# Weight products in runs of six, and score products queued behind the output of the head ahead

## The chip, the cores and the metric

The kernel runs on one core of a Trainium2 chip. The metric is the device time of one execution in microseconds. The engines are named as the profile names them: PE (TensorE), DVE (VectorE), ACT (ScalarE), POOL (GpSimd) and SP (SyncE, whose queue issues the weight loads).

## The reference

One step of a decoder trunk with four layers, for 256 prompt tokens and 8 x 4 sample tokens, which share all weights (288 columns together). Each layer is two half-weighted SwiGLU FFNs around a token mixer:

```
for i in range(4):
    x = x + 0.5 * swiglu(rms(x), ffn_w_in[i, 0], ffn_w_out[i, 0])
    x = x + mixer[i % 3](rms(x))          # 0 attention, 1 gated delta rule, 2 linear recurrence
    x = x + 0.5 * swiglu(rms(x), ffn_w_in[i, 1], ffn_w_out[i, 1])
```

The mixers are sliding-window attention with sinks (layers 0 and 3), a gated delta rule, called GDN here (layer 1), and a gated linear recurrence, HGRN (layer 2). The recurrence, per head of 128 x 128 state and in chunks of 32 tokens, is

```
attn = einsum('bhid,bhjd,bhijd->bhij', qc, kc, decay)
o = einsum('bhik,bhkv->bhiv', qc * exp(bcum), s) + einsum('bhij,bhjv->bhiv', attn, vc)
s = s * exp(bcum[-1]) + einsum('bhjk,bhjv->bhkv', kc * exp(b_last - bcum), vc)
```

followed by an RMS norm of o per head, a gate and the output weights. States of prompt and samples are outputs too. All is fp32.

## The kernel before

**Weight products.** A weight times the 288 columns is made in a form close to fp32: each weight tile is split into a high and a low part (ACT, L71, and DVE, L72, from a raw tile that SP loads, L54), each activation too, and a k-tile takes three matmuls of 128x288 (L97, L98, L99: high by high, high by low, low by high). Class `Stream` holds all weights of the program as a list of jobs in order; `st.run(n)` emits the next n jobs, four k-tiles (12 products) in most. There are 16152 products, in four layers of FFN, mixer, FFN.

**Order.** The kernel is written in an order that does not interleave; a scheduler does that. Each instruction has a priority, its place in the text, and code inside `tc.high_priority(PRIO)` (PRIO is 5000) is moved ahead of it. The mixers' units of small matmuls stand under such a priority, so that the scheduler takes an instruction of a unit when it is due and fills the time between with products. The order per engine is then fixed; an engine waits at its next instruction.

**PSUM.** Eight banks: three `acc` for the products, two `ma`, and one each of `c0`, `c1` and `s` for the mixers' small matmuls. A product that begins a new accumulator needs a free `acc`.

**GDN.** `core_unit` makes for pairs of heads the chunked rule: the inverse of the 64 x 64 triangles (L735 to L877 and on), and then for each chunk in turn L1181 (products with the state), L1182/L1183 on DVE and ACT, L1186 (new values), L1187 on ACT, L1190 and L1192 (state and output), L1195 on DVE, which updates the state that the next L1181 reads. L1140 updates the sample states.

**HGRN.** `run` emits the set-up, 56 jobs of the input weights, then under high priority the heads 0 to 3, eight jobs, heads 4 to 7, eight jobs. The in-projection has 768 products, the out-projection twice 96; the first 96 need the gates of heads 0 to 3. Per head:

- `head_scores(h)`: the state of the head is loaded by SP (two buffers); `factors` multiplies the decays of 2, 4, 8, 16 and 32 tokens (L1366, L1370, DVE); from them the scaled K on DVE and Q on POOL, level by level (L1386 to L1404, tiles `W`, 14 buffers). Then 51 score matmuls of 32x32 in bank c0 (L1415), masks and sums on DVE (L1419 to L1425), block matrices `bd` on POOL (L1427, L1430), and, in c0 again, the transposes of K (L1436, L1437) with a copy on ACT (L1439).
- `head_states(h)`: chunk sums (L1459, banks c1 and s), the chain of states SS on DVE (L1463, L1465), the output `po` in c1 (L1470, L1474, L1478, L1479), its squares on ACT (L1483), mean on DVE (L1485), the inverse square root as a power on POOL (`root`, L276), the scale on ACT (L1488), the sample states (L1492 in s and then c1, L1494 on DVE), and the output's transposes in s (L1499 to L1501).
- `gate(h)`: L1505 on DVE (heads 0 to 3) or POOL, L1506 on ACT, L1507 on DVE.

The heads are called as

```
head_scores(0)
for h in range(a, a + 4):
    if h < 7:
        head_scores(h + 1)
    head_states(h)
    gate(h)
```

Of the kernel before, what the change touches and what calls it, by code (L numbers as in the profile page):

```python
# [15 lines left out]
T = 288  # L16
# [8 lines left out]
class Stream:  # L25
# [3 lines left out]
    def __init__(self, tc, raw, split, psum):  # L29
        self.tc, self.nc, self.raw, self.split_pool, self.psum = tc, tc.nc, raw, split, psum  # L30
        self.chunks, self.jobs = [], []
        self.loaded, self.tiles, self.left = 0, {}, {}
        self.nsplit, self.parts = 0, {}
        self.njob = 0
        self.accs = {}
        self.pooled = set()
        self.held, self.mms, self.tags = [], [], {}
        self.loads = {}
        self.first = 0

# [44 lines left out]
    def run(self, count, hold=False):  # L85
        self.mms = []
        for j in range(self.njob, self.njob + count):
            self.split_to(j + 1 + AHEAD)
            chunk, view, nk, xs, acc, start, stop, evac, m = self.jobs[j]
            hi, lo = self.parts.pop(j)  # L90
            if start:
                self.accs[acc] = self.psum.tile([128, 512], F32, tag=self.tags.pop(acc, "acc"), name="acc")
            ps = self.accs[acc][:m, :T]
            mm = self.nc.tensor.matmul
            last = len(xs) - 1
            for i, (xh, xl) in enumerate(xs):
                mm(ps, hi[:, i, :m], xh(), start=start and i == 0, stop=False)  # L97
                mm(ps, hi[:, i, :m], xl(), start=False, stop=False)  # L98
                self.mms.append(mm(ps, lo[:, i, :m], xh(), start=False, stop=stop and i == last).ins)  # L99
            self.njob += 1  # L100
            if stop and hold:
                self.held.append((evac, self.accs.pop(acc)))
            elif stop:
                evac(self.accs.pop(acc))
# [7 lines left out]
def trunk(ctx: ExitStack, tc: tile.TileContext, I, consts, O):  # L112
# [1168 lines left out]
    def hgrn(i, j):  # L1281
# [91 lines left out]
        def head_scores(h):  # L1373


            kh, qh, fh = k[h], q[h], f[h]
            s0 = slice(32 * (h % 4), 32 * (h % 4) + 32)
# [7 lines left out]
            Q[1] = mx(T, "W", 14)  # L1385
            G.tensor_tensor(out=Q[1], in0=qh, in1=fh, op=ALU.mult)  # L1386
            for s in (2, 4, 8, 16, 32):
                n = T if s <= 4 else 256
                K[s], Q[s] = mx(T, "W", 14), mx(256, "qb", 2) if s == 32 else mx(T, "W", 14)
# [16 lines left out]
            kd, t4 = K[32], four(K[4], "k4t")  # L1406
# [27 lines left out]
            ps = misc("c0")  # L1434
            for c in range(2):
                PE.transpose(ps[:, c * 128:c * 128 + 128], kd[:, c * 128:c * 128 + 128], ident)  # L1436
            PE.transpose(ps[:, 256:384], t4, ident)  # L1437
            H["kdt"] = mx(256, "kdt", 2)
            S.activation(out=H["kdt"], in_=ps[:, 0:256], func=AF.Copy)  # L1439
            H["k4"] = mx(128, "k4", 2, dt=F32R)  # L1440
            hilo(H["k4"], ps[:, 256:384], ((32, 32), (96, 32)))

        def head_states(h):
# [35 lines left out]
            PE.matmul(po[:, 256:384], bd[s0, 256:384], L["vs"][s0, h // 4], start=False, stop=True)  # L1479
# [6 lines left out]
            root(r, v)  # L1486
# [3 lines left out]
            for e in range(0, 8, 4):  # L1490
                ps = misc(("c1", "s")[e // 4])
                PE.matmul(ps, H["k4"], v4m[:, e:e + 4].rearrange("p b v -> p (b v)"))  # L1492
                for a in range(4):
                    V.scalar_tensor_tensor(out=sta[:, e + a], in0=sta[:, e + a], scalar=H["ends"][:, (e + a) // 2, a % 2:a % 2 + 1],  # L1494
                                           in1=ps[:, a * 128:a * 128 + 128], op0=ALU.mult, op1=ALU.add)
            nc.sync.dma_start(out=O[11][j, :, h].rearrange("b k v -> k b v"), in_=sta)
            ps = misc("s")
# [23 lines left out]
        def run():  # L1521
# [3 lines left out]
            for a in (0, 4):  # L1525
                with tc.high_priority(PRIO):
                    if a == 0:
                        head_scores(0)
                    for h in range(a, a + 4):
                        if h < 7:  # L1530
                            head_scores(h + 1)
                        head_states(h)
# [225 lines left out]
```

## Time and profile before

| | |
|---|---|
| time of three runs | 2638.28, 2638.93, 2644.87 us (median 2638.93) |
| the profiled execution | 2632.71 us, span 2630.9 us |
| busy: PE, DVE, ACT, POOL | 2549.8 (97%), 1763.5 (67%), 1414.1 (54%), 246.4 us (9%) |
| mean granted clock of PE | 0.989 |
| DMA | 400.15 MB, mean 152 GB/s |
| stretches of the mixers | layer 0 some 20 to 380, GDN 700 to 1170, HGRN 1600 to 1870, layer 3 2200 to 2440 us |

An "idle before" or a wait names what released the engine. The clock is a share of full speed, so that a stretch of 0.89 has 22% of its time at half speed. In a timeline the duration of a matmul runs to its modelled end, and matmuls overlap: the time of one is the distance from its start to the next start.

### The profile page before, as it was taken

How to read it: one execution, taken by the hardware profiler on the slowest of the kernel's cores; microseconds unless marked ns; L12 is line 12 of the kernel's file. 1: busy time of each engine (PE TensorE's matmuls, PEld its weight loads, DVE VectorE, ACT ScalarE, POOL GpSimd, SP SyncE). 2: the span in 40 equal slices, each digit the busy share in tenths (PEclk: the TensorE clock that was granted, in tenths of full speed). 3: DMA queues.
4: the chain of work that ended last, by engine and by line, in shares of the span. 5: the costliest groups of instructions: out<-in, count | busy, mean ns of one | idle time of the engine just before them, and what ended most of it. 6: DMA issues, size and time to landing. Idle time of an engine off the chain costs nothing.

```text
span 2630.9 us, 52770 instructions
## 1 busy us (share of the span) xinstructions
PE 2549.8 (97%) x20268; PEld 2411.8 (92%) x20268; DVE 1763.5 (67%) x3772; ACT 1414.1 (54%) x3129; POOL 246.4 (9%) x404
## 2 busy tenths in 40 slices
PE   8999999999998899999999999888999999999998
PEld 8999799999997776789999999677999999979998
DVE  6666776576567867667666666877765766667655
ACT  5555655455455456755555545665554555465543
POOL 1000000000002135410000000443000000010000
PEclk9999999999999999999999999999999999999999
DMA  6655245555553354455555555333555565534553
GB/s 188 196 168 172 65 143 164 165 168 161 166 163 97 109 152 136 136 176 159 167 163 163 168 163 160 106 119 122 164 165 164 164 202 177 168 94 121 161 168 124
DMA packets 442609, 400.15 MB, mean 152 GB/s; under 512 B 24730, under 2 KB 440212, under 8 KB 442356
## 3 DMA queue, kind: packets, MB, share of 16 engines
q1 hardware_dynamic: 441732, 395.66, 49.9%
q8 instruction: 159, 2.61, 0.4%
q10 hardware_dynamic: 624, 1.11, 0.1%
q14 instruction: 94, 0.77, 0.1%
HBM read 374.64 MB, written 22.07 MB: 151 GB/s over the span
## 4 chain that ended last, share of the span: by engine, by line
PE 78%; issue 11%; DVE 6%; POOL 2%; ACT 2%; DMA 1%; DVEq 0%; POOLq 0%; ACTq 0%; SPq 0%
PE acc L97 23%; PE acc L99 23%; PE acc L98 23%; DVE lo L72 1%; PE s L545 1%; PE c L530 1%; PE c L1186 0%; DVE W L1400 0%; PE ma L537 0%; PE c L1190 0%; DVE F L1366 0%; PE c L1192 0%; PE c L1181 0%; PE c L1474 0%; ACT hi L71 0%
## 5 line engine op out<-in xcount | busy, mean ns | idle before, releaser
L97 PE MATMUL acc<-sl,hi 128*128 128x288 f32 x5384 | 1612.4, 300 | 13.0 <-ACT sl L1506 2.8
L98 PE MATMUL acc<-sl,hi 128*128 128x288 f32 x5384 | 1606.1, 298 | 1.8 <-DVE sl L1507 1.8
L99 PE MATMUL acc<-sl,lo 128*128 128x288 f32 x5384 | 1600.8, 298 | 2.4 <-DVE lo L72 2.4
L71 ACT ACTIVATE hi<-raw 128x512 fp32r<-128x512 f32 (+1 forms) x1378 | 854.3, 621 | 963.0 <-PE acc L98 934.4
L72 DVE TENSOR_TENSOR lo<-raw,hi 128x512 fp32r<-128x512 f32 (+1 forms) x1378 | 948.4, 689 | 571.2 <-ACT hi L71 515.1
L97 PEld LDWEIGHTS acc<-sl,hi 128*128 128x128 f32 x5384 | 1016.4, 189 | 26.2 <-issue 11.5
L99 PEld LDWEIGHTS acc<-sl,lo 128*128 128x128 f32 x5384 | 1021.2, 190 | 14.6 <-issue 10.0
L98 PEld LDWEIGHTS acc<-sl,hi 128*128 128x128 f32 x5384 | 1018.9, 189 | 12.8 <-issue 9.2
L276 POOL TENSOR_TENSOR r<-v,roots 128x3 f32<-128x3 f32 x5 | 5.8, 1164 | 1847.2 <-DVE v L296 1847.2
L366 DVE TENSOR_TENSOR sil<-acc,sil 128x288 f32<-128x288 f32 x176 | 79.7, 456 | 54.8 <-PE acc L99 51.3
L359 DVE TENSOR_TENSOR sil<-acc,rbc 128x288 f32<-128x288 f32 x176 | 79.6, 456 | 50.1 <-PE acc L99 49.8
L368 DVE TENSOR_TENSOR sl<-sil,sl 128x288 fp32r<-128x288 f32 x176 | 78.9, 452 | 0.0
L360 ACT ACTIVATE sil<-sil 128x288 f32<-128x288 f32 x176 | 77.6, 445 | 2.1 <-DVE sil L359 2.0
L367 ACT ACTIVATE sl<-sil 128x288 fp32r<-128x288 f32 x176 | 77.6, 445 | 0.0
L700 DVE SCALAR_TENSOR_TENSOR acc<-buf,cw,acc 128x312 f32<-128x312 f32 x96 | 59.0, 625 | 11.9 <-ACT acc L698 11.5
L246 ACT ACTIVATE sl<-x,gT 128x288 fp32r<-128x288 f32 x96 | 51.0, 536 | 26.2 <-DVE x L383 15.3
L249 DVE SCALAR_TENSOR_TENSOR sl<-x,gT,sl 128x288 fp32r<-128x288 f32 x96 | 50.5, 530 | 0.1
L262 ACT ACTIVATE sq<-x 128x288 f32<-128x288 f32 x91 | 38.7, 430 | 5.1 <-DVE x L383 5.1
L515 ACT ACTIVATE e<-e,m 128x128 f32<-128x128 f32 (+1 forms) x72 | 32.6, 454 | 16.1 <-DVE m L512 15.8
L1131 POOL TENSOR_TENSOR st<-st,ex 128x512 f32<-128x512 f32 x32 | 37.4, 1190 | 18.1 <-PE ma L1098 18.1
L259 DVE TENSOR_TENSOR ssq<-ssq,sq 128x288 f32<-128x288 f32 x84 | 37.8, 450 | 0.1
L512 DVE CUSTOM_DVE_ANT_0 e<-c,sl,sink 128x128 f32<-128x128 f32 (+1 forms) x72 | 27.8, 418 | 10.6 <-PE c L530 7.7
(435 smaller groups left out, 1823.3 us busy)
## 6 DMA issues: line engine op xcount, KB each, us to landing
raw<-in_ffn_w_in_dram SPq DMA_DIRECT2D x352, 512.0 KB
raw<-in_ffn_w_out_dram SPq DMA_DIRECT2D x128, 512.0 KB
raw<-in_ffn_w_out_dram SPq DMA_DIRECT2D x64, 384.0 KB
raw<-in_gdn_w_in_dram SPq DMA_DIRECT2D x48, 512.0 KB
raw<-in_hgrn_w_in_dram SPq DMA_DIRECT2D x32, 512.0 KB
out_dram<-st SPq DMA_DIRECT2D x24, 512.0 KB
raw<-in_swa_w_in_dram SPq DMA_DIRECT2D x32, 256.0 KB
raw<-in_swa_w_out_dram SPq DMA_DIRECT2D x32, 256.0 KB
```

Of the source, the lines that this page charges most:

```text
L71: self.nc.scalar.activation(out=h, in_=src, func=AF.Copy)
L72: (self.nc.gpsimd if j in self.pooled else self.nc.vector).tensor_tensor(out=l, in0=src, in1=h, op=ALU.subtract)
L97: mm(ps, hi[:, i, :m], xh(), start=start and i == 0, stop=False)
L98: mm(ps, hi[:, i, :m], xl(), start=False, stop=False)
L99: self.mms.append(mm(ps, lo[:, i, :m], xh(), start=False, stop=stop and i == last).ins)
L246: S.activation(out=h[m], in_=x[:, m], func=AF.Identity, scale=g)
L359: V.tensor_tensor(out=t, in0=ps[:, :T], in1=nrm[key]["rbc"], op=ALU.mult)
L360: S.activation(out=t, in_=t, func=AF.Silu)
L366: V.tensor_tensor(out=t, in0=ps[:, :T], in1=t, op=ALU.mult)
L367: S.activation(out=h, in_=t, func=AF.Copy)
L368: V.tensor_tensor(out=l, in0=t, in1=h, op=ALU.subtract)
L700: V.scalar_tensor_tensor(out=a[:, 0:312], in0=b[:, t:t + 312], scalar=cw[:, 32 * t + mt:32 * t + mt + 1], in1=a[:, 0:312], op0=ALU.mult, o ...
```

## The change

Three things. `Stream.run` gives products a priority of their own: of each pair of k-tiles, the first product keeps the place it had, and the other five follow at three times PRIO, above the units, so that products come in runs of six in the whole program. In HGRN, `head_scores` is split: `head_factors(h)` loads the state and makes the factors, for heads 0 and 1 first and for head h + 2 behind head h; `head_scores(h)` makes the transposes of K first and then the scores, and is held on PE behind a given matmul: behind the job `first + 18` for head 0, behind the last output matmul of head h for head h + 1 (`issue_after`). And in `head_states` the root on POOL becomes `rsqrt`, eleven DVE operations with the mean (a bit shift, a subtraction and three Newton steps of three); the sample states are made in two halves, both in bank s, the second in `head_rest` behind the next scores, with the output's transposes, now in c1. The tiles `W` get 20 buffers.

```diff
@@ -34,9 +34,10 @@
         self.pooled = set()
-        self.held, self.mms, self.tags = [], [], {}
+        self.held, self.mms, self.tags, self.ends = [], [], {}, {}
         self.loads = {}
         self.first = 0
+        self.follow = 3 * PRIO
...
@@ -94,9 +95,13 @@
             for i, (xh, xl) in enumerate(xs):
-                mm(ps, hi[:, i, :m], xh(), start=start and i == 0, stop=False)
-                mm(ps, hi[:, i, :m], xl(), start=False, stop=False)
-                self.mms.append(mm(ps, lo[:, i, :m], xh(), start=False, stop=stop and i == last).ins)
+                with self.tc.high_priority(i % 2 * self.follow):
+                    mm(ps, hi[:, i, :m], xh(), start=start and i == 0, stop=False)
+                with self.tc.high_priority(self.follow):
+                    mm(ps, hi[:, i, :m], xl(), start=False, stop=False)
+                    self.mms.append(mm(ps, lo[:, i, :m], xh(), start=False, stop=stop and i == last).ins)
+            self.ends[j] = self.mms[-1]
             self.njob += 1
...
@@ -1370,11 +1375,9 @@
-        def head_scores(h):
+        def head_factors(h):
             kh, qh, fh = k[h], q[h], f[h]
-            s0 = slice(32 * (h % 4), 32 * (h % 4) + 32)
             H = L["h", h] = {}
...
@@ -1382,11 +1385,11 @@
             K, Q = {1: kh}, {}
-            Q[1] = mx(T, "W", 14)
+            Q[1] = mx(T, "W", 20)
             G.tensor_tensor(out=Q[1], in0=qh, in1=fh, op=ALU.mult)
...
                 n = T if s <= 4 else 256
-                K[s], Q[s] = mx(T, "W", 14), mx(256, "qb", 2) if s == 32 else mx(T, "W", 14)
+                K[s], Q[s] = mx(T, "W", 20), mx(256, "qb", 2) if s == 32 else mx(T, "W", 20)
                 if s == 2:
...
@@ -1403,7 +1406,22 @@
                             in1=L["tok8"].rearrange("p (e t) -> p e t", e=8), op=ALU.mult)
-            kd, t4 = K[32], four(K[4], "k4t")
+            H["K"], H["Q"], H["t4"] = K, Q, four(K[4], "k4t")
+        def head_scores(h):
+            kh, qh, H = k[h], q[h], L["h", h]
+            K, Q, kd, t4 = H.pop("K"), H.pop("Q"), None, H.pop("t4")
+            kd = K[32]
+            s0 = slice(32 * (h % 4), 32 * (h % 4) + 32)
+            ps = misc("c0")
+            for c in range(2):
+                PE.transpose(ps[:, c * 128:c * 128 + 128], kd[:, c * 128:c * 128 + 128], ident)
+            PE.transpose(ps[:, 256:384], t4, ident)
+            H["kdt"] = mx(256, "kdt", 2)
+            S.activation(out=H["kdt"], in_=ps[:, 0:256], func=AF.Copy)
+            H["k4"] = mx(128, "k4", 2, dt=F32R)
+            hilo(H["k4"], ps[:, 256:384], ((32, 32), (96, 32)))
             ps = misc("c0")
...
@@ -1431,14 +1449,6 @@
             H["bd"] = bd
-            ps = misc("c0")
-            for c in range(2):
-                PE.transpose(ps[:, c * 128:c * 128 + 128], kd[:, c * 128:c * 128 + 128], ident)
-            PE.transpose(ps[:, 256:384], t4, ident)
-            H["kdt"] = mx(256, "kdt", 2)
-            S.activation(out=H["kdt"], in_=ps[:, 0:256], func=AF.Copy)
-            H["k4"] = mx(128, "k4", 2, dt=F32R)
-            hilo(H["k4"], ps[:, 256:384], ((32, 32), (96, 32)))
...
@@ -1476,25 +1486,34 @@
                 PE.matmul(po[32 * a:32 * a + 32, 256:384], qm[:, 32 * e:32 * e + 32], sta[:, e], start=False, stop=False)
-            PE.matmul(po[:, 256:384], bd[s0, 256:384], L["vs"][s0, h // 4], start=False, stop=True)
+            L["po"] = PE.matmul(po[:, 256:384], bd[s0, 256:384], L["vs"][s0, h // 4], start=False, stop=True).ins
             ssq, v, r = sm(3, "gs"), sm(3, "gv"), sm(3, "gf")
...
             V.tensor_scalar(v, ssq, 1.0 / 128, EPS, ALU.mult, ALU.add)
-            root(r, v)
+            rsqrt(r, v, ssq)
             for c in range(3):
...
                              scale=r[:, c:c + 1])
-            for e in range(0, 8, 4):
-                ps = misc(("c1", "s")[e // 4])
+            L["rest", h] = sta, H, v4m, o
+            sample_states(h, (0,))
+        def sample_states(h, parts):
+            sta, H, v4m = L["rest", h][0:3]
+            for e in parts:
+                ps = misc("s")
                 PE.matmul(ps, H["k4"], v4m[:, e:e + 4].rearrange("p b v -> p (b v)"))
...
                                            in1=ps[:, a * 128:a * 128 + 128], op0=ALU.mult, op1=ALU.add)
+        def head_rest(h):
+            sample_states(h, (4,))
+            sta, H, v4m, o = L.pop(("rest", h))
             nc.sync.dma_start(out=O[11][j, :, h].rearrange("b k v -> k b v"), in_=sta)
-            ps = misc("s")
+            ps = misc("c1")
             for c in range(2):
...
@@ -1525,11 +1544,18 @@
                     if a == 0:
-                        head_scores(0)
+                        head_factors(0)
+                        head_factors(1)
+                        with tc.issue_after(st.ends[first + 18]):
+                            head_scores(0)
                     for h in range(a, a + 4):
+                        head_states(h)
                         if h < 7:
-                            head_scores(h + 1)
-                        head_states(h)
+                            with tc.issue_after(L["po"]):
+                                head_scores(h + 1)
+                        head_rest(h)
+                        if h < 6:
+                            head_factors(h + 2)
                         gate(h)
...
```

Lines move: L97, L98, L99 are L100, L102, L103 in the changed kernel; the core units' L1181, L1186, L1190, L1192 are L1186, L1191, L1195, L1197, and L1140 is L1145. In HGRN L1415 is L1433, L1436 and L1437 are L1419 and L1420, L1459 is L1469, L1470 to L1479 are L1480 to L1489, L1492 is L1507.

TensorE in HGRN, around the scores of the seventh head. Before, the scores (L1415) stand ahead of the output of the head before (L1470 and on, `po`), and the transposes of K behind:

```order
L1415 MATMUL c_22556<-W 32x32 x33
L1415 MATMUL c_22556<-W,sl 32x32 x9
L1415 MATMUL c_22556<-sl 32x32 x9
L1470 MATMUL c_22660<-sl,bd 128x128
L1474 MATMUL c_22660<-SS,qb 32x128 x3
L1470 MATMUL c_22660<-sl,bd 128x128
L1474 MATMUL c_22660<-SS,qb 32x128
L99 MATMUL acc<-sl,lo 128x288
L97 MATMUL acc<-sl,hi 128x288
L98 MATMUL acc<-sl,hi 128x288
L1436 MATMUL c_22618<-cst,W 128x128 x2
L1437 MATMUL c_22618<-cst,k4t 128x128
```

Changed, around the scores of the sixth head: the transposes (L1419, L1420), a run of six and a sample state (L1507) ahead of the scores (L1433). The last output matmul of the head ahead, L1489, stands two rows above:

```order
L1419 MATMUL c_22481<-cst,W 128x128 x2
L1420 MATMUL c_22481<-cst,k4t 128x128
L1353 MATMUL ma<-cst,v 128x128 x2
L100 MATMUL acc<-sl,hi 128x288
L102 MATMUL acc<-sl,hi 128x288
L103 MATMUL acc<-sl,lo 128x288
L100 MATMUL acc<-sl,hi 128x288
L102 MATMUL acc<-sl,hi 128x288
L103 MATMUL acc<-sl,lo 128x288
L1507 MATMUL s<-v4m,k_22133 128x512
L1433 MATMUL c_22491<-W 32x32 x33
L1433 MATMUL c_22491<-W,sl 32x32 x9
```

The scores moved from before the output of the head ahead to behind it, the transposes from behind the scores to before them.

TensorE in GDN, the core unit of a pair of heads before (`co` is the state, `u` the new values, `w` and `km` belong to the sample states):

```order
L1140 MATMUL ma<-w_11998,km 128x256 x4
L98 MATMUL acc<-sl,hi 128x288
L1186 MATMUL c_12407<-u,sl 64x128 x2
L99 MATMUL acc<-sl,lo 128x288
L97 MATMUL acc<-sl,hi 128x288
L1140 MATMUL ma<-w_11998,km 128x256
L1190 MATMUL c_12407<-u 128x128
L1190 MATMUL s<-u 128x128
L1192 MATMUL c_12407<-u,sl 64x128 x2
L1140 MATMUL ma<-w_11998,km 128x256 x3
L98 MATMUL acc<-sl,hi 128x288
L99 MATMUL acc<-sl,lo 128x288
```

Changed, a stretch of the same unit:

```order
L1195 MATMUL c_12407<-u 128x128
L1195 MATMUL s<-u 128x128
L1197 MATMUL c_12407<-u,sl 64x128 x2
L1130 MATMUL ma<-wp,a_11994 128x128 x2
L1145 MATMUL ma<-w_11998,km 128x256 x2
L1186 MATMUL c_12407<-co,sl 64x128 x4
L1145 MATMUL ma<-w_11998,km 128x256 x4
L1191 MATMUL c_12407<-u,sl 64x128 x2
L1145 MATMUL ma<-w_11998,km 128x256 x2
L1195 MATMUL c_12407<-u 128x128
L1195 MATMUL s<-u 128x128
L1197 MATMUL c_12407<-u,sl 64x128 x2
```

Products that stood between the steps of the unit stand ahead of it and behind it; in this stretch the steps follow each other.

## Rows read from the trace of the kernel before

**Rows 1.** The page: the span, and the chain that ended last by engine.

```profile
span 2630.9 us, 52770 instructions
...
PE 78%; issue 11%; DVE 6%; POOL 2%; ACT 2%; DMA 1%; DVEq 0%; POOLq 0%; ACTq 0%; SPq 0%
```

**Rows 2.** Stretches: width, busy time of five engines, PEclk, DMA share, GB/s.

```profile
20.00:380.00 360.00, 356.97 (x2679) 338.16 (x2678) 243.64 (x577) 193.61 (x421) 13.92 (x23) 0.99 0.51 152
400.00:450.00 50.00, 50.00 (x377) 50.00 (x376) 31.69 (x55) 25.62 (x47) 0.00 (x0) 1.00 0.55 164
700.00:1170.00 470.00, 442.08 (x3848) 374.22 (x3847) 327.13 (x827) 269.43 (x750) 129.39 (x243) 0.98 0.48 138
...
1600.00:1870.00 270.00, 240.85 (x2438) 209.81 (x2437) 208.17 (x477) 164.66 (x456) 83.85 (x109) 0.97 0.42 128
```

**Rows 3.** Waits of PE, 1640 to 1850 us: total, times, longest.

```profile
PE c L1415 <- DVE W L1400: 5.7, 4, 3.0
PE c L1415 <- POOL W L1400: 5.5, 2, 2.9
PE c L1436 <- DVE at L1422: 3.9, 4, 1.4
PE s L1499 <- ACT o L1488: 2.9, 7, 0.5
```

**Rows 4.** Stretches, PE alone: width, busy time, PEclk, DMA share, GB/s.

```profile
1640.00:1670.00 30.00, 23.07 (x332) 0.89 0.28 86
1740.00:1750.00 10.00, 6.18 (x133) 0.87 0.39 112
1830.00:1850.00 20.00, 16.14 (x99) 0.83 0.32 104
850.00:950.00 100.00, 87.70 (x978) 0.91 0.44 121
950.00:1160.00 210.00, 200.67 (x1603) 1.00 0.52 147
```

**Rows 5.** Timeline of PE behind the gates of HGRN: start, duration, instruction.

```profile
1835.17 0.44 PE L97 MATMUL acc<-sl,hi 128*128 128x288 f32 x1
1835.41 0.44 PE L98 MATMUL acc<-sl,hi 128*128 128x288 f32 x1
```

**Rows 6.** Timeline of PE in the core units of GDN.

```profile
963.22 0.29 PE L97 MATMUL acc<-sl,hi 128*128 128x288 f32 x1
963.44 0.66 PE L1181 MATMUL c<-co,sl 128*64 128x128 f32 x8
964.03 0.40 PE L98 MATMUL acc<-sl,hi 128*128 128x288 f32 x1
964.26 0.29 PE L99 MATMUL acc<-sl,lo 128*128 128x288 f32 x1
964.39 0.40 PE L1140 MATMUL ma<-w,km 128*128 128x256 f32 x2
964.63 0.29 PE L97 MATMUL acc<-sl,hi 128*128 128x288 f32 x1
...
966.02 0.44 PE L1186 MATMUL c<-u,sl 64*64 64x128 f32 x4 [0.56 <-ACT co L1183]
...
968.90 0.66 PE L1181 MATMUL c<-co,sl 128*64 128x128 f32 x8
```

**Rows 7.** Waits of PE, 700 to 1170 us.

```profile
PE c L1186 <- ACT co L1183: 4.0, 8, 1.3
```

**Rows 8.** Groups by line, 1640 to 1850 us: busy, mean ns, idle before.

```profile
L276 POOL TENSOR_TENSOR gf<-gv,roots 128x3 f32<-128x3 f32 x8 | 6.8, 851 | 26.2 <-DVE gv L1485 26.2
...
L1424 DVE TENSOR_REDUCE at<-am 128x64 f32<-128x384 f32 x8 | 6.6, 820 | 0.2
...
L1485 DVE TENSOR_SCALAR gv<-gs 128x3 f32<-128x3 f32 x8 | 1.3, 162 | 0.9 <-ACT o L1483 0.9
```

**Rows 9.** Stretch from the first head's output to the eighth's, columns of rows 2.

```profile
1678.40:1815.60 137.20, 120.11 (x1404) 94.95 (x1402) 106.72 (x277) 90.73 (x292) 52.75 (x72) 0.99 0.42 127
```

## The prediction

> **What bounds the kernel now.** I read the page first: of a span of 2630.9 us PE carries 78% of the chain that ended last [rows 1], so only what TensorE does, waits for, or does at a lower clock can change the time. The second view is a table of stretches [rows 2]. In the FFN stretch the engine has no idle time and starts 377 matmuls in 50 us, nearly all of them weight products, one each 133 ns. There are 16152 products, 16152 x 0.1333 = 2153 us that the change does not touch: it neither adds nor removes a product. The mixer stretches show where PE idles: 360.0 - 357.0 = 3.0 us in the first attention layer, 470.0 - 442.1 = 27.9 in the GDN layer, 270.0 - 240.9 = 29.1 in the HGRN layer. So the 57 us of idle time in two layers are what a better order can reach.
>
> The third view names the waits of PE in the HGRN layer [rows 3]. Score products (L1415) wait 5.7 + 5.5 = 11.2 us for the factors W that DVE and POOL make (L1400), and the transposes behind them (L1436) wait 3.9 us for the masking of the scores (L1422, reading the scores), because all of these use the single bank c0. The output transposes (L1499) wait 2.9 us, seven times, for the scaled output, the last step behind the square root.
>
> The fourth view is the granted clock in pieces of this layer [rows 4]: 0.89, 0.87 and 0.83 in three pieces and 1.00 between them. A clock of 0.89 over 30 us is 6.6 us at the half rate (30 x 0.11 / 0.5), 0.87 over 10 us is 2.6, 0.83 over 20 us is 6.8. At the half level (1.2 of 2.4 GHz) a product takes 0.24 us [rows 5] and not 0.133, so a microsecond there does the work of 0.55. The first two of the three pieces begin behind a wait of the scores (3.0 and 2.9 us are the longest two of L1415 in [rows 3]); the third stands where the output weights' products wait for the gates of the last head.
>
> The fifth view is a timeline of PE [rows 6], which prices an interruption of the products. L97 to L1181 is 0.22 us where product to product is 0.13, and L98, the first product behind the eight L1181, takes 0.23 to the next: 0.19 us are lost on top of the small matmuls' own time. The two L1140, of the full shape 128*128, cost only their own 0.24 us: the step from L99 to them is 0.13, and L97 follows at once. So an interruption costs 0 or about 0.19 us, by its kind.
>
> **The change, part by part.**
>
> *Runs of six (all layers).* By the order written out for both kernels the small matmuls interrupt the products 346 times before and 220 times after: 100 to 58 in the two attention layers, 155 to 90 in GDN, 77 to 58 in HGRN, 13 elsewhere, unchanged. Of those that go I count about 0.3 in attention, 0.55 in GDN and 0.7 in HGRN as of the kind that costs 0.19 [rows 6]; rounded, 42 x 0.055 = 2.3 us, 65 x 0.10 = 6.5 and 19 x 0.13 = 2.5. Bounds: 0 and 126 x 0.19 = 24 us. Sum of this part: -11.3.
>
> *What the runs do to the units of GDN.* A high-priority run of six can only start when its accumulator is free. In the new order, three times (at the tile boundaries 6000, 6096 and 6192 of the program's products) 17, 32 and 36 rows of small matmuls stand with no product between; the longest such stretch was 11 rows. Their chain runs through ACT and DVE: L1181 to L1186 to the next L1181 is 966.02 - 963.44 + 968.90 - 966.02 = 5.5 us per step [rows 6], which products hid. In the longest stretch three steps, 16.5 us, stand over about 14 us of PE work; with the wait at its end some 4.5 us are bare, over the three stretches about 9. Against that L1186's present waits of 4.0 us [rows 7] and other small ones shrink where units are kept together, about 5. Net +4; bounds -5 and +9. The part before them, where the inverses are made, follows DVE's chain in both kernels, and DVE's work there stays: 0.
>
> *HGRN: factors one head ahead.* The scores of head h+1 find their factors made, so the 11.2 us of L1415 go. Moving the transposes of K ahead of the scores takes them out of the queue behind the masks: 3.9 us go. What is late next: the first head has only 6 products between its scores and its output while its mask, two reductions (the longer 0.82 us, L1424 in [rows 8]) and block matrices need some 3 us, +2; the output transposes wait for a longer square root (below), +1; the state sums on DVE meet factors more often, +1.5. Idle: -15.1 + 4.5 = -10.6, from 29.1 to 18.5. Bounds: -15.1 and 0, if each wait returns elsewhere.
>
> *HGRN: the clock.* Of the 16 us at the half rate the 9.2 behind score waits go; the 6.8 at the gates stay. 9.2 x 0.45 = -4.1. Bounds 0 and -7.
>
> *HGRN: square root on DVE.* One POOL operation of 851 ns becomes ten more DVE operations of 128x3, each like L1485's 162 ns [rows 8]: 1.6 us of DVE per head and 13 us over eight. Between the outputs of the first and the last head DVE is busy 106.7 of 137.2 us [rows 9]; it becomes 106.7 + 7 x 1.6 = 118. So DVE could let the heads go down to 118 us and no further: the gain in this stretch has a ceiling of 19 us, and my terms for it (about 13 of the 17 us of this layer) stay below. It is therefore costed at nothing, apart from the +1 above; if the cover is gone, each microsecond is worth one. The rows show 162 ns for 3 columns beside 820 for the 384 of L1424, so a small operation is mostly fixed cost. The Trainium skill, Perfetto Trace Analysis, in its section on optimizing Scalar and DVE operations, gives a fixed overhead of about 60 ns to an SBUF operation on DVE and advises grouping small ones; by it this edit goes the wrong way, and at 60 ns it would cost 5 us of DVE, an estimate, in place of 13. The measured 162 ns is used.
>
> *The rest of the diff.* More W buffers (14 to 20), the second half of the sample states behind the next scores, and output transposes in c1 free bank s earlier. The state load of a head still stands on SP behind the store of the head two before, whose buffer it takes, and weight loads stand behind it as now; the DMA share there is 0.42 [rows 9]: 0. The gates stand where they stood, between input and output products: 0.
>
> Sum: -11.3 + 4 - 10.6 - 4.1 = -22 us. The profiled execution is 2632.7 us (span 2630.9 and 1.8 around it), so 2611; the median shown, 2638.9, is 6.2 above the profiled one, so the forecast for a median is **2617 us**.
>
> **The rivals.**
>
> *A, DVE becomes the pace of the HGRN heads.* For: 118 us of work in what should become about 124, in chains, with POOL and DVE alternating on the factors; DVE's own delays come back as waits of the state products. Against: DVE idles 30 us there now. If the heads gain 3 us in place of 13, the sum is -12, 2627.
>
> *B, slower: the product-free stretches in GDN cost the clock.* From 950 to 1160 us the clock is 1.00 now [rows 4]; in the stretches at 850 to 950, with many small matmuls and a long wait, it is 0.91. If three stretches of about 14 us each, bare of products, bring the clock of 50 us to the half level, 50 x 0.45 = 22 us come on top of +9 of idle in place of +4: -22 + 22 + 5, and if the heads gain little too, another +10: 2632 to 2653. It decides once the clock of GDN's core falls below about 0.90. The Trainium skill, Perfetto Trace Analysis, section on matmul optimizations, speaks for it: the engine scales its power with utilization, and matmuls should run back to back. By that rule the longer runs of products help and the longer runs of small matmuls hurt; the row at 950 to 1160 shows 1.00 with interruptions everywhere, so nothing here bears the hurt out yet.
>
> *C, the change does not do what it says.* The waits of the scores turn into waits of the output transposes (2.9 us now) and of L1470, and an interruption costs nothing where it was followed by a wait: gain 0 to 6 us, 2633 to 2639.
>
> **The numbers.** About 0.3% (8 us) is what a measurement of this kernel can tell from no change. Forecast -22 (between -35 and -13): 0.58. A: 0.20, mostly faster by over 8 us. C: 0.13, no change. B: 0.09, of which most is slower or the same. Faster 0.74, same 0.18, slower 0.08. The low end takes the full idle and clock terms with GDN at -5: 2638.9 - 37 = 2602. The high end takes in A and C: 2640.
>
> **What would show it.** In the changed profile L1415's counterpart no longer waits for L1400's and PE's idle time in the HGRN layer is near 18 us, with the clock at 1.00 but for the gates; that layer is shorter by about 17 us. GDN is shorter by 2 or 3, its idle up by about 4 with the waits of the chain L1186, L1191, L1195 at three places; attention shorter by about 1 each. I am wrong if the clock of GDN's core drops, if DVE is over 95% busy through the heads, or if the idle time of HGRN stays at 29.

## The result and the profile after

The changed kernel takes 2670.64 us (2665.49 to 2673.48, four runs) against 2640.31 us (2638.28 to 2644.87, four runs): ratio 1.011, interval [1.0097, 1.0123]. It is 30 us slower. Forecast was a median of 2617 us, 22 us less, with a range of 2602 to 2640.

The page of the changed kernel: the span, then the granted clock in 40 slices, where the 7s and 8s stand in GDN, and the chain.

```profile
span 2671.6 us, 52860 instructions
...
PEclk9999999999998977799999999999999999999999
...
PE 79%; issue 11%; DVE 6%; POOL 2%; ACT 1%; DMA 1%; POOLq 0%; DVEq 0%; ACTq 0%; SPq 0%
```

The chain has the shares of [rows 1], and PE is as busy as before (97% of the span): neither tells of the loss. The stretches do. The same columns as [rows 2], with GDN and HGRN where they now lie:

```profile
20.00:380.00 360.00, 356.94 (x2703) 339.26 (x2702) 245.97 (x583) 195.04 (x426) 14.78 (x23) 0.99 0.51 153
400.00:450.00 50.00, 50.00 (x378) 50.00 (x377) 31.34 (x55) 25.61 (x47) 0.00 (x0) 1.00 0.54 163
700.00:1210.00 510.00, 472.17 (x3803) 396.23 (x3802) 319.58 (x821) 269.06 (x745) 119.84 (x243) 0.88 0.44 126
1640.00:1910.00 270.00, 240.74 (x2432) 209.45 (x2431) 211.64 (x560) 163.54 (x455) 82.22 (x101) 0.95 0.42 127
```

Clock 0.88 over 510 us of GDN, where [rows 2] had 0.98 over 470. Split at the middle of the GDN layer, first the changed kernel, then the one before (PE alone, columns of [rows 4]):

```profile
777.00:977.00 200.00, 179.29 (x1724) 0.88 0.41 113
977.00:1200.00 223.00, 206.06 (x1426) 0.82 0.42 119
```

```profile
777.00:977.00 200.00, 180.85 (x1806) 0.96 0.43 121
977.00:1200.00 223.00, 214.24 (x1692) 1.00 0.53 151
```

At 0.88 and 0.82, 200 x 0.12 / 0.5 + 223 x 0.18 / 0.5 = 128 us are at the half level; before it was 16. At the prediction's price of 0.45 us for a microsecond at the half level, the 112 us more cost 112 x 0.45 = 50 us, an estimate. I also timed the layers by the start of their first weight product in the two traces, which gives the table that the rest uses (us; behind the stroke, what of it was at the half clock):

| | before | after |
|---|---|---|
| attention, both | 243.5 / 17.1 | 237.4 / 13.7 |
| GDN, products 5232 to 6000 | 199.1 / 17.1 | 204.6 / 48.9 |
| GDN, 6000 to 6792 | 223.5 / 0 | 264.0 / 77.4 |
| HGRN | 238.9 / 17.1 | 239.9 / 27.3 |
| the eight FFNs (the last one to its last product), each within 0.4 us of before | 211.6 to 215.4 / 0 | 211.6 to 215.3 / 0 |

GDN +46.1, HGRN +1.0, attention -6.1: but for some 0.3 us these are the 40.7 us by which the two profiled spans differ (2671.6 - 2630.9). The medians differ by 30, because the profiled execution of before (2632.71 us) is faster than all its timed ones, and that of the changed kernel (2673.44) is near the top of its own.

By an estimate, a layer's time can be taken apart into PE's idle time, 0.45 us for each microsecond at the half level, and the rest, which is work and the price of interruptions (us, before and after):

| | idle | half level x 0.45 | rest |
|---|---|---|---|
| GDN, first part | 19.2, 20.9 | 7.7, 22.0 | 172.3, 161.7 |
| GDN, second part | 8.8, 16.9 | 0, 34.8 | 214.8, 212.3 |
| HGRN | 29.1, 29.3 | 7.7, 12.3 | 202.1, 198.3 |
| attention, both | 5.8, 4.6 | 7.7, 6.1 | 230.0, 226.6 |

So GDN lost some 49 us by the clock and 10 by idle time. The rest fell by 13, which fits the fewer interruptions of its products but is not shown to be theirs.

What the clock follows is to be seen in the timeline of PE in the changed kernel, at one of the three stretches that the prediction found in the order:

```profile
1013.82 0.29 PE L100 MATMUL acc<-sl,hi 128*128 128x288 f32 x1
...
1014.22 0.40 PE L1145 MATMUL ma<-w,km 128*128 128x256 f32 x2
1015.86 0.74 PE L1145 MATMUL ma<-w,km 128*128 128x256 f32 x4 [1.24 <-POOL km L1140]
...
1018.38 0.69 PE L1191 MATMUL c<-vt,sl 64*64 64x128 f32 x4
...
1024.66 1.12 PE L1186 MATMUL c<-co,sl 128*64 128x128 f32 x8
...
1034.96 0.79 PE L1145 MATMUL ma<-w,km 128*128 128x256 f32 x2 [1.24 <-POOL km L1140]
...
1041.95 0.53 PE L1191 MATMUL c<-vt,sl 64*64 64x128 f32 x4
1042.41 0.40 PE L100 MATMUL acc<-sl,hi 128*128 128x288 f32 x1
1042.65 0.29 PE L102 MATMUL acc<-sl,hi 128*128 128x288 f32 x1
```

From 1014.2 to 1042.4 us no product runs. The eight records of L1186 take 1.12 us where the same instructions took 0.66 in [rows 6]; behind 1042.4 the products follow at 0.13 us again. The stretch, 14 us of work as I had counted it, lasts 28; of the other two, the one at product 6192 lasts 29 us and the one at 6000 lasts 11. In it the bare waits that I had priced are there (1.24, 1.24 and shorter ones) and are the smaller part.

In HGRN the waits of the scores and of the transposes of K in [rows 3] are gone, and others stand in their place (waits of PE in the changed kernel, 1640 to 1910 us):

```profile
PE acc L103 <- DVE lo L73: 12.4, 9, 2.9
PE c L1469 <- ACT vm L1463: 4.1, 1, 4.1
PE c L1480 <- DVE SS L1475: 2.7, 3, 1.5
...
PE c L1518 <- ACT o L1498: 1.8, 3, 1.2
```

No score waits for its factors. The products wait 12.4 us for the low parts of the weights, and PE's idle time in the layer is 29 us as before, where 18.5 was forecast.

### The profile page after: what moved, and what is told of

Read it like the earlier page. It is cut to its first block, busy times and chain, and to the rows that moved or that the text cites. A ratio compares the mean times of both kernels' runs of the same rounds, so it can differ in the third digit from the quotient of the medians.

```text
span 2671.6 us, 52860 instructions
## 1 busy us (share of the span) xinstructions
PE 2581.3 (97%) x20268; PEld 2437.0 (91%) x20268; DVE 1756.5 (66%) x3860; ACT 1411.0 (53%) x3129; POOL 234.8 (9%) x396
## 4 chain that ended last, share of the span: by engine, by line
PE 79%; issue 11%; DVE 6%; POOL 2%; ACT 1%; DMA 1%; POOLq 0%; DVEq 0%; ACTq 0%; SPq 0%
PE acc L100 24%; PE acc L103 22%; PE acc L102 22%; DVE lo L73 1%; PE c L535 1%; DVE st L1509 1%; PE c L1186 1%; PE c L1191 1%; PE c L1195 1%; PE s L550 1%; PE c L1197 0%; DVE W L1403 0%; PE ma L542 0%; POOL st L1136 0%; PE ma L1145 0%
## 5 line engine op out<-in xcount | busy, mean ns | idle before, releaser
L100 PE MATMUL acc<-sl,hi 128*128 128x288 f32 x5384 | 1627.3, 302 | 16.9 <-DVE sl L1225 6.4
L103 PE MATMUL acc<-sl,lo 128*128 128x288 f32 x5384 | 1594.7, 296 | 12.8 <-DVE lo L73 12.8
L102 PE MATMUL acc<-sl,hi 128*128 128x288 f32 x5384 | 1599.1, 297 | 0.7 <-DVE sl L1526 0.7
L100 PEld LDWEIGHTS acc<-sl,hi 128*128 128x128 f32 x5384 | 1020.1, 190 | 43.6 <-issue 28.4
L103 PEld LDWEIGHTS acc<-sl,lo 128*128 128x128 f32 x5384 | 1024.0, 190 | 16.2 <-DVE lo L73 15.9
L102 PEld LDWEIGHTS acc<-sl,hi 128*128 128x128 f32 x5384 | 1021.9, 190 | 4.8 <-issue 2.6
L705 DVE SCALAR_TENSOR_TENSOR acc<-buf,cw,acc 128x312 f32<-128x312 f32 x96 | 52.9, 576 | 12.7 <-ACT acc L703 12.5
L387 DVE TENSOR_TENSOR res<-acc,rh 128x288 f32<-128x288 f32 x64 | 29.0, 453 | 40.7 <-PE acc L103 40.7
L520 ACT ACTIVATE e<-e,m 128x128 f32<-128x128 f32 (+1 forms) x72 | 32.6, 454 | 17.7 <-DVE m L517 16.9
L1136 POOL TENSOR_TENSOR st<-st,ex 128x512 f32<-128x512 f32 x32 | 35.5, 1129 | 16.9 <-PE ma L1103 16.9
```

The source lines that it names most:

```text
L705: V.scalar_tensor_tensor(out=a[:, 0:312], in0=b[:, t:t + 312], scalar=cw[:, 32 * t + mt:32 * t + mt + 1], in1=a[:, 0:312], op0=ALU.mult, o ...
```

## The experiments

Each is compared with runs of the kernel before on the same chip; medians of before lie between 2639.9 and 2641.5 us.

**First: which part loses?** The runs of six alone, in the kernel before:

```diff
+                with self.tc.high_priority(i % 2 * self.follow):
+                    mm(ps, hi[:, i, :m], xh(), ...)
+                with self.tc.high_priority(self.follow):
...
```

> The kernel before with the runs of six alone (priority of products in the whole program), HGRN as it was. Theory S (the runs push GDN's products ahead of its units, which leaves stretches of small matmuls without a product, and in these the clock falls to the half level): GDN takes about 46 us more than before, as in the changed kernel, the attention layers 6 us less together, HGRN within 5 us of before; 2670 to 2685 us in all. Rival H (the loss comes from the HGRN part or from its larger buffers moving the tiles of other layers): GDN as before, 2630 to 2640 us.

Measured: 2663.97 us (2661.96 to 2666.04), 1.0092 [1.0077, 1.0107]. GDN 204.7 and 264.1 us, as in the changed kernel; HGRN 229.6, 9 shorter than before, which puts the total 6 us under theory S's range. The loss is in the products' edit.

The HGRN part, with the priority of the runs 0 (`self.follow = 0`):

> The changed kernel with the priority of the runs set to 0, so the HGRN part alone. Theory S: GDN within 3 us of before with its clock at 1.00 between 950 and 1160 us, attention as before. In HGRN, theory D (the root on DVE makes the low parts of the weights late): PE still waits some 10 us for the low parts, HGRN gains 0 to 4 us, 2634 to 2640. Theory R (the runs make the low parts late, since products come in bursts that DVE's splits at low priority don't follow): those waits fall to about 2 us, HGRN gains 10 to 17 us, 2622 to 2630. Rival H: the loss of 30 us stays, 2665 or more.

Measured: 2675.21 us (2673.75 to 2687.18), 1.0145 [1.0119, 1.0170]. GDN took 454.9 us without a run of six, so theory S fell, and H, which has the total right, is at odds with the run above it. In HGRN theory D held (239.4 us, the products still wait 12.9 us for low parts), and R fell.

The changed kernel with `st.follow = 0` from the start of GDN to its end:

> The changed kernel with the runs of six off in GDN alone. Theory S: GDN as before (about 423 us against 469), attention 6 us shorter than before, HGRN as in the changed kernel (about before): 2632 to 2636. Rival: if the waits in GDN come from somewhere else in the change, GDN stays over 445 us and the total over 2655.

Measured: 2665.98 us (2649.77 to 2672.24), 1.0089 [1.0057, 1.0121]. A miss of the same kind: the second part of GDN took 256.4 us with no run of six in it.

The same with `root(r, v)` for `rsqrt(r, v, ssq)`:

> As the run with the runs of six off in GDN, and the inverse square root of HGRN on POOL again in place of DVE's eleven operations. Theory D: the wait of products for low parts in HGRN falls from 12 us to under 5, HGRN 6 to 10 us shorter, 2623 to 2628. Theory R: no change beyond 3 us.

Measured: 2655.71 us (2652.59 to 2661.30), 1.0066 [1.0045, 1.0087]. Some 10 us less than the run before it, HGRN 230.5 against 239.6 us; 17.1 against 27.3 us of it at the half clock make some 4.6 of the 9. The wait for low parts, which theory D had at under 5 us, is still 11.5, so the gain is not that wait's.

**What was left in these kernels.** A block of priority 0 is not nothing. The scheduler numbers instructions by a counter, and a block of `high_priority` sets the counter back at its end, so that the products inside it take no numbers. Read at every 300th job while the two programs are written, the counter stands at

```
job            300    600    900   1200
plain         4733   9111  13185  17205
in blocks     1205   2043   2613   3126
```

Between jobs 300 and 600, which hold GDN, 4378 numbers became 838. The units' distances (PRIO of 5000 and those of GDN, up to 6500) are counted in these numbers, and now reach past everything that is left of the program. So units go ahead of products that they used to be mixed with. This was theory C, and two kernels tell the counter from the runs.

The runs of six alone, the counter kept:

```diff
                     self.mms.append(mm(ps, lo[:, i, :m], xh(), ...).ins)
+                self.tc.cur_priority += 3
```

> The kernel before with the runs of six alone, and with the scheduler's counter of priorities moved on by 3 for each k-tile, as the plain products moved it. Theory C (what changes the order in GDN is the counter: a block of high priority sets it back at its end, so the products no longer count, and every priority given as a distance reaches several times as far into the program): GDN's longest stretch without a product is 23 rows in its second part as written out, its clock is 1.00 between 950 and 1160 us or nearly, GDN 418 to 428 us, HGRN near 230 and attention 4 to 6 us shorter than before: 2615 to 2628. Theory P (the priority of the runs themselves): GDN over 445 us, 2645 or more.

Measured: 2625.69 us (2623.18 to 2627.43), 0.9944 [0.9928, 0.9961]: 14 us faster than before. Second part of GDN 224.7 us, so theory C held. The first part is another matter: it keeps 47.8 us at the half level (205.0 us in all) with the counter kept. There the runs themselves make the stretches without a product longer; three that lasted 5.5 to 6.4 us before last 11 to 14.

The counter alone: the blocks around the products, `self.follow = 0`, no other edit.

> The kernel before with each product inside a block of priority 0, which changes no priority distance in itself but sets the counter back; no runs of six, HGRN as it was. Theory C: GDN has the stretches of 74 and 78 rows without a product and takes some 455 us, the attention layers some 3 us more each, 2665 to 2680. Theory P: as before, 2636 to 2644.

Measured: 2674.44 us (2670.65 to 2681.78), 1.0135 [1.0117, 1.0154]. The total is in theory C's range, but not all of it is GDN (460.7 us): in the profiled execution, the longest of the four, the eight FFNs take some 13 us more than before, at the full clock, as they do in the other kernel with plain products and the counter set back. The stretches in GDN (PE, columns of [rows 4]), first with runs and the counter kept, then with the counter set back and no runs:

```profile
777.00:977.00 200.00, 178.44 (x1715) 0.88 0.41 113
977.00:1200.00 223.00, 214.99 (x1725) 0.99 0.54 152
```

```profile
777.00:977.00 200.00, 180.99 (x1769) 0.92 0.44 122
977.00:1200.00 223.00, 202.82 (x1442) 0.86 0.43 120
```

As written out, the longest stretch without a product in the second part, counted in matmuls (a row of the order can hold several), is 26 before, 23 in the first of these and 78 in the second (86 in the changed kernel); where it is short the clock is 1.00 or 0.99. The four cases, medians in us:

| | counter kept | counter set back |
|---|---|---|
| plain products | 2640.0 | 2674.4 |
| runs of six | 2625.7 | 2664.0 |

Runs of six gain 14 and 10 us, the counter loses 34 and 38. This is shown, and it carries the result. With runs of six the counter's loss is all in GDN (468.8 against 429.8 us), as in the changed kernel.

**Is it the clock, and what does the clock follow?** Work is added in the core units of the changed kernel, its output overwritten:

```diff
+                for _ in range(6):
+                    PE.matmul(ps[:, 256:384], ident, ktok[:, 0:128])
                 for hf, cl in hfs:
                     PE.matmul(ps[hf, 256:384], A[hf, xa], rhs[hf])
```

> The changed kernel with work added: in each of the 32 steps of GDN's core units six matmuls of 128x128 whose output the next matmul overwrites, so the result is the same. If the clock falls because PE executes too little in the stretches between the products (theory S), the clock in 977 to 1200 us rises from 0.82 to 0.90 or more and the added work costs less than its own time, total 2655 to 2680. If the clock falls for another reason (a share of small matmuls, power), the clock stays or falls and the added work is paid at the half rate, 2700 or more.

Measured: 2686.47 us (2684.07 to 2688.25), 1.0169 [1.0153, 1.0185]. The stretches:

```profile
777.00:977.00 200.00, 179.05 (x1767) 0.91 0.42 113
977.00:1200.00 223.00, 211.61 (x1689) 0.95 0.39 110
```

With matmuls of full shape among the narrow ones the clock of the second part rose from 0.82 to 0.95, the time at the half level there from 77 to 21 us, as theory S had it. The total is 6 us above its bound: the added work cost 16 us more than the clock gave back. The added matmuls also moved others in the order, so the run does not show the clock alone. Taken apart as above, GDN has 48 us more of work (the 384 records of the added matmuls take 52 us from start to next start), 32 less for the clock (126 us at the half level became 55) and 5 less of idle time: the sum is the 10 us by which GDN is longer than in the changed kernel, and it bears out the price of the clock.

**The whole change with the counter kept**, by the same line:

> The whole change, with the scheduler's counter moved on by 3 for each k-tile as in the run of the runs of six with the counter kept. Theory C: the loss in GDN goes (second part 225 us against 264, clock 0.99), and what is left is the gain of the runs, 14 us, with the HGRN part worth -5 to +7 on it: 2621 to 2633. If the two parts of the change disturb each other elsewhere, over 2645.

Measured: 2637.95 us (2632.23 to 2642.38), 0.9986 [0.9973, 1.0000]. GDN 203.2 and 226.1 us: the counter's loss is gone. But 12 us of the 14 that the runs gave are gone too, in HGRN: 244.8 us, against 230.7 with the runs and the old HGRN; of these 14 us, 8 are the clock's (34.1 against 17.1 us at the half level) and 6 idle time (31.0 against 25.3).

**HGRN by itself.** The HGRN part with plain products (the loop of before), all other layers in the order of before, and the same with the root on POOL:

> The kernel before with the whole HGRN part of the change and plain products. All other layers stand in the same order as before, so GDN and attention are as before. The prediction's sum for this part: HGRN 10 to 17 us shorter, 2622 to 2630. Theory D (the root on DVE takes the gain back): HGRN within 4 us of before, 2634 to 2642.

> As the run with the HGRN part and plain products, with the inverse square root on POOL as before. Theory D: HGRN 6 to 12 us shorter than in that run, 2624 to 2632. If the root is innocent: within 3 us of that run.

Measured: 2641.73 us (2635.36 to 2646.46), 1.0005 [0.9993, 1.0016], and 2640.93 us (2636.93 to 2645.59), 1.0007 [0.9997, 1.0016]. The part is worth nothing with plain products. The first run has theory D's time, but the second shows that the root is not its cause here. Waits of PE in the first of these, 1600 to 1880 us:

```profile
PE acc L99 <- DVE lo L72: 11.5, 12, 2.9
PE ma L1349 <- DVE v L1301: 2.6, 5, 0.9
...
PE c L1476 <- DVE SS L1471: 2.2, 3, 1.3
```

The waits for low parts can be taken away: splits of HGRN's weights at a priority above the heads (`st.first = 2 * PRIO` around HGRN's jobs).

> The HGRN part with plain products, and the splits of HGRN's weights given priority over its heads, as GDN's first part gives it. Theory L (the waits for scores were exchanged for waits for low parts, since the factors made ahead on DVE stand in front of the splits): the 11.5 us of PE's waits for L72 fall below 4, HGRN is 6 to 10 us shorter than in the run without the priority, 2630 to 2636. Rival W (DVE has no slack there, so what waits changes and the sum doesn't): the waits return at the states or the scores, within 3 us, 2638 to 2644.

Measured: 2643.39 us (2637.68 to 2645.64), 1.0005 [0.9995, 1.0015]. The wait for low parts fell to 4.2 us, the time did not, so theory L fell; the waits moved on, to the values and the states (waits of PE, 1610 to 1880 us):

```profile
PE ma L1349 <- DVE v L1301: 10.4, 6, 2.7
PE c L1476 <- DVE SS L1471: 5.9, 3, 2.4
PE acc L99 <- DVE lo L72: 4.2, 5, 1.5
```

Is it the amount of DVE's work, or the order? Thirty splits on POOL (`st.pooled.update(range(first + 20, first + 80, 2))`):

> The HGRN part with plain products, and every second split of the weights in the heads' stretch on POOL, 30 of them, some 20 us of DVE's work moved. Theory W in its strong form (the amount of DVE's work sets the pace): the heads gain about 10 us, 2628 to 2634. Theory Q: waits for low parts may fall, the sum stays within 3 us of that without, 2638 to 2644.

Measured: 2657.66 us (2656.52 to 2658.74), 1.0059 [1.0044, 1.0074], 16 us slower, with HGRN at 250.1 us, outside both ranges. It settles little: POOL was the wrong place, since a split takes longer there and the products wait 4.4 us for those splits. Groups by line from 1680 to 1830 us:

```profile
L72 POOL TENSOR_TENSOR lo<-raw,hi 128x512 fp32r<-128x512 f32 x19 | 25.1, 1319 | 37.7 <-ACT hi L71 37.2 <-POOL bd L1444 0.4
...
L1441 POOL TENSOR_TENSOR bd<-at,lmask 128x128 f32<-128x128 f32 x14 | 7.2, 532 | 22.2 <-DVE gf L273 16.9 <-DVE at L1438 5.2
```

And the queueing taken out: scores again before the states of the head ahead, factors still a head ahead, root on POOL.

```diff
-                        head_states(h)
                         if h < 7:
-                            with tc.issue_after(L["po"]):
-                                head_scores(h + 1)
+                            head_scores(h + 1)
+                        head_states(h)
```

> Plain products, factors a head ahead and root on POOL, but the scores of a head stand before the states of the head ahead again, with nothing queued behind an output. Theory Q (the queueing makes a serial chain per head): HGRN 6 to 10 us shorter than with the queueing (some 232 us against 239), 2630 to 2636. Theory W (DVE and PE pass the waits between them whatever the order): within 3 us of it, 2638 to 2643.

Measured: 2639.70 us (2634.23 to 2644.59), 0.9992 [0.9982, 1.0002]: no difference with plain products, so theory Q fell.

**A version that beats both.** Runs of six outside GDN (where their blocks still set the counter back), plain products inside it, HGRN as it was:

> Runs of six outside GDN, plain products inside it (GDN's order is that of before, row by row), HGRN as it was. GDN as before (some 425 us), attention 4 to 6 us shorter together, HGRN 8 us shorter: 2624 to 2630. If the first part of GDN loses by the runs (205 us with them, 199 to 204 without), 3 to 5 us faster than the runs with the counter kept: 2620 to 2624.

Measured: 2623.40 us (2619.77 to 2626.96), 0.9935 [0.9916, 0.9954]. With the HGRN part (root on POOL), and with its queueing taken out:

> Runs of six outside GDN, plain products inside it, the HGRN part with the root on POOL. As the best version so far but for the HGRN part: 2620 to 2627 if that part is worth nothing, as it was with plain products; 2612 to 2618 if it gains once the products come in runs.

> As the run before, with the scores in their old place before the states and nothing queued. Theory Q: 6 to 10 us faster than with the queueing, 2612 to 2618. Theory W: the same as with it.

Measured: 2629.56 us (2627.19 to 2630.84), 0.9951 [0.9937, 0.9966], and 2623.41 us (2619.61 to 2630.86), 0.9933 [0.9911, 0.9954]. The medians differ by 6 us, with intervals that overlap, and that is not shown to be the queueing: in the two profiles HGRN differs by 2.3 us (231.0 and 228.6), and GDN, whose order is the same in both, by 3.5. Without the queueing the HGRN part is worth nothing. So the 17 us under the kernel before come from the blocks of six outside GDN, mostly in attention and HGRN.

## Why the prediction was wrong

**Runs of six, -11.3 us: right in the sum, not in its parts.** They gain 14.3 us with the counter kept, and 10.5 with it set back. HGRN's 8 us are more than the 2.5 that I gave it: there the runs also shortened waits, and the scores' waits for W fell from 11.2 to 9.6 us in that run. GDN, which had 6.5 of the 11.3, gained nothing: 429.8 us, where nine profiles with the order of before have 422.6 to 432.3. The rest of its first part fell by some 10 us (172 to 161.5), and the clock took them back. That the sum came out is partly luck. (The counts in it add up to 345 and 219, one less than written.)

**"Net +4; bounds -5 and +9" for GDN: this is the step that failed.** I had found the stretches of 17, 32 and 36 rows in the order, and summed their waits at the full clock; the layer took 46 us more in the profiled pair. The idle time rose by 10, near the bound of +9; the clock, which this step put at nothing, cost some 49, and the rest of the layer fell by 13. The stretch itself I had counted in work, 14 us, without asking what clock such work gets. Two pointers were in the rows. [Rows 4] had 0.91 in the only stretch with many small matmuls and 1.00 where products were mixed in; I read the second as evidence against the fall, though its order was just what the change took away. And I wrote the stretches down to the runs of six, waiting for an accumulator. That cause was wrong: in the second part, where the three stretches are, runs with the counter kept have no such stretch (23 matmuls at most, clock 0.99), and the counter without runs has them (78, clock 0.86). The diff says nothing of the counter, and the order had said only that something moved.

**Rival B was the case, at 0.09.** Its mechanism (stretches without products, half clock) is what happened, its place was right, its price was half: it took 50 us at the half level, and 112 were found, since the three stretches last 69 us in place of 42 and since the first part of the layer, with the inverses, lost its clock too (16 to 48 us). The second of these is the runs' own doing: it is 47.8 us with the counter kept, and 17 to 38 with the order of before. The rule of the Trainium skill that I set beside it (Perfetto Trace Analysis, section on matmul optimizations: matmuls back to back in batches, since the engine scales its power with utilization) agrees with the run with added matmuls: 0.82 to 0.95.

**HGRN, "Idle: -15.1 + 4.5 = -10.6" and "-4.1" for the clock: wrong in what replaces the waits.** The mechanism was right as far as the scores: no score waits for its factors. But alone the part gives 1.0005, and the time at the half clock rose from 17 to 27 us in the changed kernel, and the idle time stayed at 29, which I had named as a sign of being wrong. My 4.5 for "what is late next" left out the products' own splits, which stand behind the heads' work on DVE: 12.4 us. Taking those away moved the waits to the values and the states. With DVE busy 121.1 of 151.0 us between the first and the eighth output in the changed kernel, DVE idles 30 us there, of which it waits 23 for PE, and PE idles 20, of which it waits some 13 for DVE. So rival A's direction was right, and its measure (118 of about 124 us) was not. What sets the pace of a head stays open: neither the root, nor the priority of the splits, nor the queueing moved the time by itself with plain products.

**The root on DVE, "costed at nothing".** The root is eleven operations beside the mean, not ten (and not eleven with it, as the section on the change has it). They take 5.4 + 5.0 + 3.7 + 1.3 + 1.3 = 16.7 us, 2.1 per head, against 13 and 1.6 forecast (groups by line of the changed kernel, 1680 to 1890 us):

```profile
L277 DVE SCALAR_TENSOR_TENSOR gf<-gs,gf 128x3 f32<-128x3 f32 x24 | 5.4, 225 | 0.1
L276 DVE TENSOR_TENSOR gs<-gs,gv 128x3 f32<-128x3 f32 x24 | 5.0, 208 | 0.2
L275 DVE SCALAR_TENSOR_TENSOR gs<-gf 128x3 f32<-128x3 f32 x24 | 3.7, 155 | 0.3
L273 DVE TENSOR_SCALAR gf<-gf 128x3 int32<-128x3 int32 x8 | 1.3, 164 | 0.1
...
L272 DVE TENSOR_SCALAR gf<-gv 128x3 int32<-128x3 int32 x8 | 1.3, 162 | 0.0
```

The Trainium skill, Perfetto Trace Analysis, in its section on optimizing Scalar and DVE operations, has about 60 ns as the fixed overhead of such an operation, a busy time, and puts the latency in a profile at about twice that; here one took 155 to 225 ns from its start to its end, which is more.

With plain products the root's place is worth under 1 us, with runs of six 10 us in the one pair that differs by it alone. The range of that pair's first run (2649.77 to 2672.24) is too wide to call it shown by the totals. The layer's own time speaks for it: with runs of six HGRN took 237.3 to 244.8 us in the four profiles with the root on DVE (the changed kernel, with work added, with the runs off in GDN, with the counter kept), 228.6 to 231.0 in the three with the HGRN part and the root on POOL, and 229.6 to 230.7 in the three with the old HGRN. So once the products come in runs, "costed at nothing" was likely wrong by some 9 us, about half of it the clock's; by which chain of waits is not shown.

**The rest.** Attention gained 6.1 us in the profiled pair against 2.3 forecast, 1.5 of it from the clock, which also differs between kernels with the same order.

## What to carry to other kernels

When an edit puts instructions into a priority block, look first at what the block does to the numbering of everything else: a block of priority 0 around each product, which reads as no change, cost 34 us here. When a new order has stretches in which the large matmuls are missing, price them at the half clock as the first guess, not as a rival, and look for the clock in the stretch of the old trace that is most like them. And a wait that is removed between two engines that wait for each other in turn is worth nothing until the next wait in the chain has been found.

## What the runs showed of the hardware

The clock of a stretch differs between executions of one and the same order. Nine of the profiled kernels have GDN's matmuls in the order of before, row by row. Its first part took 199.1 to 207.3 us in them, with 17.1 to 37.5 at the half level; with the idle time and 0.45 us for each microsecond at the half level taken off, 171.4 to 172.3 are left in all nine. So a few microseconds of a single profile are the clock's own, and the price of 0.45 holds for this mix of matmuls too.

PE can have work nearly all the time and lose its clock. In the second part of GDN it was busy in 206.06 of 223 us with the clock at 0.82, where two long stretches of small matmuls (57 us together) had no product in them, and in 214.24 us at 1.00, where products stood between the same matmuls. A split of 128x512 takes 1319 ns on POOL, and 784 on DVE in the run with all splits there.
